# Two repeated gather inputs kept in DRAM, fewer gathers in flight, and a new pace of row steps

## The chip, the cores and the metric

The kernel runs on one core of a Trainium2 chip. A core has a matrix engine (TensorE, PE in the profile), a vector engine (VectorE, DVE), an activation engine (ScalarE, ACT), a general engine (GpSimd, POOL) and a queue engine that only issues DMAs (SyncE, SP). Sixteen DMA engines move data between DRAM (HBM) and the on-chip memory SBUF; TensorE writes to PSUM. Each engine works through its own list of instructions in order and waits on semaphores for the others. The metric is the device time of one execution, in microseconds (us); lower is better.

## What is computed

One layer of a streaming encoder with 512 frames of width 2048 and 16 meta tokens. The first half is attention; it is not touched here. The second half is PEER, a layer with 16384 experts, each one row `u` and one row `v` of 2048 numbers. Every token scores two sets of 128 keys for each of 8 heads, takes the best 16 of each, then the best 16 of the 256 sums, and so has 8 x 16 = 128 experts with weights `g`:

```python
q = (xb @ w_q).reshape(PEER_BLOCK, PEER_HEADS, 2, PEER_HALF)
s = jnp.einsum('thcd,hcnd->thcn', q, sub_keys)
...
h = jnp.einsum('tkd,td->tk', u[idx], xb)
act = (g * jax.nn.gelu(h, approximate=False))
return jnp.einsum('tk,tkd->td', act, v[idx])
```

Everything is float32. A product of two float32 matrices is made of three TensorE products of a high and a low half (`mm3`, lines 259 to 261): low x high, high x low, high x high.

## The kernel before

**Two ways through PEER.** The 512 frames are split. 328 of them (`ND`) go through *all* experts as dense products: a first pass over 128 blocks of `u` (`u_products`), then a second pass over 256 tiles of `v`. The other 184 frames are done with *gathers*: an indirect DMA on GpSimd's queue (line 1042) fetches 128 rows of `u` or `v`, one to each partition (1 MB), and VectorE works on them (a "row step"; line 1055 for `u`, lines 1061 and 1063 for `v`). The 184 frames are four parts, `NS = 128, 32, 16, 8`. For the first each partition holds one frame, and 128 gathers serve its 128 experts. The others have fewer frames than partitions, so each frame's input row is repeated over 4, 8 or 16 partitions, and they take 32, 16 and 8 gathers. That makes 184 row steps on `u` and 184 on `v`. In the list `todo` they stand in one order; the first `NU = 200` are done during the score stage and the first pass, the other 168 during the second pass.

**The repeated inputs.** The inputs of the three small parts are written once to DRAM (`xn_d`, 56 rows, line 1143). `copies(dst, t0, n)` (line 936) reads `n` of these rows so that each is repeated 128/n times, and fills 128 partitions. It is called for part 1 (32 rows) into the tile `xgb`, in the score stage; for part 2 (16 rows) into `lists`, when the routing steps, which use `lists` for their tables, are over; and for part 3 (8 rows) into `lists` again, 8 row steps after parts 0 to 2 are through. All three go out on SP's queue, as do the weight tiles.

**Weight tiles.** `front`, `wtile` and `load` (lines 232 to 256) load a tile of 128 x 1024 (`wr`, four buffers), make its high half on ScalarE (`wh`, line 245) and its low half (`wl`, line 246) on VectorE, or on GpSimd where the call says so. `wh` and `wl` have three buffers; in the first pass and the second there are more.

**The score stage** (lines 1076 to 1174) runs over 16 key sets, here called heads `hc`. Each multiplies the 512 frames by `wq` (two tiles: the first with its low half on VectorE, the second on GpSimd, except for head 1, where both are on VectorE), scales and splits the result, and one head later forms the scores (`scores`) and picks the best 16 on VectorE (`top16`, lines 915 to 919). In head 0 the inputs `xn` of the dense part are normalised, in head 1 they are split into `hgh` and `hgl` (16 splits). At head 4 three gathers are sent, and each head from 5 on does one row step with up to three rows in flight (`row_step(..., 3)`); there are three row buffers (`bufs=3`). Heads 0 and 8 load and split a tile of keys (`skh`, `skl`).

**The first pass** runs over 128 blocks `e`. Each loads two tiles of `u`, makes the dense products of 328 frames (48 matrix instructions), and beside them come the routing of the dense frames (`route`), the gates (`gates_of`) and the row steps. `PACE` says how many row steps are done by which block (linear between its points), and `rows_due` brings the count up to it twice a block. At the turn to the second pass the memory of the first is given back, and one row in four then goes into a buffer that lies there (`gs["pool"]`). In the second pass `PACE_V` does the same over 512 pieces.

The instructions are not run in exactly the order in which they are written: within the dependences a scheduler orders each engine's list, by its own estimate of the times, with what is written earlier first. `add_manual_dep` with `NOSYNC` fixes single orders.

Of the kernel before, what the change touches and what calls it, by code (L numbers as in the profile page):

```python
# [9 lines left out]
F32 = mybir.dt.float32  # L10
# [13 lines left out]
P = 128  # L24
D = 2048
# [10 lines left out]
NK = 128  # L36
# [3 lines left out]
NS = 128, 32, 16, 8  # L40
# [175 lines left out]
def body(tc, nc, a, dbg=None):  # L216
# [73 lines left out]
    gwb_d = dp.tile([NB, P], F32, name="gwb_d")  # L290
    eob_d = dp.tile([NB, P], I32, name="eob_d")
    xn_d = dp.tile([NB, D], F32, name="xn_d")
    h_d = dp.tile([NG, P, GRP, ND], F32, name="h_d")
    g_d = dp.tile([NG, P, NBT, GRP, TH], F32, name="g_d")

# [639 lines left out]
    def copies(dst, t0, n):  # L935
        SP.dma_start(dst, xn_d[t0:t0 + n, None, :].to_broadcast([n, P // n, D]))
# [69 lines left out]


    slots = [[(i, k) for k in range(n)] for i, n in enumerate(NS)]
    NU = 200
    todo = [("u", *s) for i in range(3) for s in slots[i]]  # L1010
    todo += [("v", *s) for s in slots[0][:NU - NR]] + [("u", *s) for s in slots[3]]
    todo += [("v", *s) for s in slots[3] + slots[0][NU - NR:NU - NR + 44] + slots[2] + slots[0][NU - NR + 44:] + slots[1]]
    PACE = (0, 14, 60, 124, NK - 0.5), (11, 26, 94, 194.5, NU)
    PACE_V = (0, 64, 488), (0, 20, 2 * NR - NU)
    OWN = NU - 9
    xs, ys = [xg, xgb, lists, lists], [xg, xgb]
# [30 lines left out]
    def row_step(mark, lead):  # L1047
        n = gs["done"]
        while gs["sent"] < min(len(todo), n + lead):
            send()  # L1050
        (src, part, k), row = todo[n], rows.pop(n)
        w = acts[part][:, k:k + 1]
        if src == "u":
            assert part < 2 or gs["x"] == part
            ins = V.scalar_tensor_tensor(row, row, 1.0, xs[part], ALU.mult, ALU.mult, accum_out=w)  # L1055
        else:
            y = ys[min(part, 2)]
            if part > 1:
                row = row.rearrange("p (c d) -> p c d", d=P)
            if k == 0:  # L1060
                ins = V.tensor_scalar(y, row, w, None, ALU.mult)
            else:
                ins = V.scalar_tensor_tensor(y, row, w, y, ALU.mult, ALU.add)  # L1063
        tc.add_manual_dep(ins.ins, mark.ins.name, NOSYNC, reason="keeps the gathers spread")
        gs["done"] += 1
        if gs["done"] == sum(NS[:3]) + 8:
            gs["x"] = 3
            copies(lists, BO[3], NS[3])
        if src == "u" and k == NS[part] - 1:
            S.activation(acts[part], acts[part], AF.Gelu, scale=rcols[part])  # L1070
            V.tensor_mul(acts[part], acts[part], gws[part])
# [15 lines left out]
    with tc.tile_pool(name="score", bufs=2, side="right") as sp_:  # L1087
        raws = []

        def raw_in():  # L1090
            t = xn.tile([P, ND], F32, name="xn")
            G.dma_start(t, ht_d[len(raws)][:, :ND])
            raws.append(t)

        sk = {}
        def scores(hc, qh, ql):
            ps = ps_tile()
            skh, skl = sk["now"]
            s = slice(hc % 8 * P, (hc % 8 + 1) * P)
            for ti in range(4):  # L1100
                t = slice(ti * P, (ti + 1) * P)
                mm3(ps[:, t], qh[:, t], ql[:, t], skh[:, s], skl[:, s], True, True)
            sc = sp_.tile([P, 4, NK], F32, name="sc")
            S.activation(sc, ps.rearrange("p (t n) -> p t n", n=NK), AF.Copy)
            for ti in (3, 2, 0, 1):
                top16(v1[:, ti, hc], i1[:, ti, hc], sc[:, ti], NK)
            if hc % 4 == 3:
                for _ in range(10):
                    next(early, None)

        late = []
        wq = {(0, hf): front("wq", 0, hf, G if hf else V) for hf in range(2)}
        for _ in range(KC):
            raw_in()
        for hc in range(16):
            ps = ps_tile()
            for hf in range(2):
                wh, wl = wq.pop((hc, hf)) if (hc, hf) in wq else front("wq", hc, hf, G if hf else V)
                for k in range(8):
                    s = slice(k * P, (k + 1) * P)  # L1120
                    kk = hf * 8 + k
                    mm3(ps, wh[:, s], wl[:, s], hgh[:, kk], hgl[:, kk], kk == 0, kk == KC - 1)
                    if (hc, kk) == (0, 3):
                        rstd(rh_, rh_, SEQ, D, sp_, ("qf", "sc", "sc"))
            qh = sp_.tile([P, SEQ], F32R, name="pqh")
            ql = sp_.tile([P, SEQ], F32R, name="pql")
            qf = sp_.tile([P, SEQ], F32, name="qf")
            if hc == 0:


                for hf in range(2):
                    wq[1, hf] = front("wq", 1, hf)
                for m in range(KC):
                    V.scalar_tensor_tensor(raws[m], raws[m], gain("ffn")[:, m:m + 1], rh_[:, :ND], ALU.mult, ALU.mult)
            if hc == 1:
                for m in range(KC):
                    split(hgh[:, m, :ND], hgl[:, m, :ND], raws[m])
                normed.close()
                gs["rows"] = rt.enter_context(tc.tile_pool(name="rows", bufs=3, side="left"))
            V.tensor_mul(qf, ps, rh_)  # L1140
            if hc == 0:
                natural(*last_natural)
                S.dma_start(xn_d, xgb[:NB])
            split(qh, ql, qf)
            late.append((hc, qh, ql))
            if hc == 1:
                V.memset(rh_[:, :ND], 1.0)
            if hc == 4:
                pt_ = ps_tile()
                rr = sp_.tile([P, 4, NK], F32, name="sc")  # L1150
                T.transpose(pt_[:, :P], rh_[:, TA:], ident)
                for j, (t, n) in enumerate(zip(BC[1:], NS[1:])):
                    V.tensor_copy(rr[:, j].rearrange("p (t r) -> p t r", r=P // n), rh_[:, t, None].to_broadcast([P, n, P // n]))
                    T.transpose(pt_[:, (j + 1) * P:(j + 2) * P], rr[:, j], ident)
                V.tensor_copy(rcol, pt_[:, :1])
                for j in range(len(NS) - 1):
                    V.tensor_copy(rcolb[:, j:j + 1], pt_[:, (j + 1) * P:(j + 1) * P + 1])
            if hc:
                scores(*late.pop(0))
            if hc == 1:  # L1160
                copies(xgb, BO[1], NS[1])
            if hc % 8 == 0:
                wr_ = raw_half()
                skh = sp_.tile([P, 1024], F32R, name="skh", bufs=1)
                skl = sp_.tile([P, 1024], F32R, name="skl", bufs=1)
                SP.dma_start(wr_, a["front"][FIDX[("sub", hc // 8, 0)]])
                split(skh, skl, wr_)
                sk["now"] = (skh, skl)
            if hc == 4:
                for _ in range(3):  # L1170
                    send()
            if hc > 4:
                row_step(more["lo"], 3)
        ahead = u_products(0)
        scores(*late.pop(0))

# [152 lines left out]
    for e in range(NK):  # L1329
        g = e // GRP  # L1330
        if e == NK // 2:
            spread_rows()
        if e == NK - 4:
            assert next(steps, steps) is steps and next(gate_steps, steps) is steps
            assert gs["done"] >= OWN
            group_in(0)
        def beside(hf):
            next(gate_steps, None)
            if hf == 0:
                rows_due(e)  # L1340
            for _ in range(hf if e < 8 else 1 if e < 24 or e % 2 else hf):
                if next(steps, steps) is steps and not gs["third"]:
                    gs["third"], gs["x"] = True, 2
                    copies(lists, BO[2], NS[2])

        if e == 0:
            ps = ahead
            for hf in range(2):
                beside(hf)
        else:  # L1350
            ps = u_products(e, beside)
        hb = up.tile([P, ND], F32, name="hb")
        more["gelu"] = S.activation(hb, ps[:, :ND], AF.Gelu)
        S.dma_start(h_d[g][:, e % GRP], hb)
        if e == NK - 2:
            gated(*held[0])
            parts = {0: [vi.tile([P, D], F32R, name=x, tag=t)[:, :GRP * ND].rearrange("p (j t) -> p j t", t=ND)
                         for x, t in (("vah", "gin"), ("val", "hin"))]}
            split(*parts[0], held.pop(0)[0])
        if e == NK - 1:  # L1360
            group_in(1)
        rows_due(e + 0.5)
# [149 lines left out]
```

## Time and profile before

| | us |
|---|---|
| median of 3 runs | 3508.65 |
| lowest, highest | 3507.4, 3513.76 |
| the profiled execution | 3506.72 |
| its span, from first to last instruction | 3504.9 |

The profile is one execution, recorded by the hardware. Its page gives busy time by engine; its views list waits by the engine that waited and what released it, instructions in order of time, the chain of work that ended last, and busy times in windows. In a window's row the clock is the share of full TensorE clock that was granted; PE counts as busy at either clock, so a lower clock has to be counted beside the idle time. The DMA share is the mean busy share of the 16 DMA engines and can pass 1 by a little. Times in rows are us from the start of the span. The score stage runs from about 1317 to 1544, the first pass to about 2546, the second to about 3490.

### The profile page before, as it was taken

What the parts mean: (1) busy time and instruction counts of PE and PEld (TensorE: products, weight loads), DVE (VectorE), ACT (ScalarE), POOL (GpSimd) and SP (SyncE); (2) the same over time, 40 slices, a digit from 0 to 9 for tenths busy, and PEclk for the clock granted to TensorE, in tenths of its full rate; (3) what the DMA queues carried; (4) which work ended last, traced back from release to release, by engine and by line L of the source; (5) the groups of instructions that cost most, each with busy time, mean ns of one, the idle gap of its engine ahead of it and who ended that gap; (6) DMA issues with size and microseconds to landing.
All of it is one profiled execution on the core that took longest, in us unless ns stands there. A gap on an engine that the chain in (4) does not pass through costs nothing.

```text
span 3504.9 us, 53419 instructions
## 1 busy us (share of the span) xinstructions
PE 3435.6 (98%) x21114; PEld 3202.8 (91%) x21114; DVE 2603.3 (74%) x3608; ACT 1420.5 (41%) x2304; POOL 758.1 (22%) x555
## 2 busy tenths in 40 slices
PE   9999999999999999999999999999989999999997
PEld 8988888888888887789999999999989999999997
DVE  5533334346754557999999988887789999999997
ACT  4232233335543223233475676665333333333333
POOL 1000000000011122322233233233212333233330
PEclk9999999999999999999999999999999999999999
DMA  5322222222144434669999999999999999999993
GB/s 172 102 97 97 100 99 94 96 99 79 43 153 138 137 134 136 223 218 338 368 391 395 366 412 412 411 404 359 374 373 367 391 406 401 394 385 398 404 385 124
DMA packets 226854, 917.84 MB, mean 262 GB/s; under 512 B 27775, under 2 KB 53487, under 8 KB 179059
## 3 DMA queue, kind: packets, MB, share of 16 engines
q1 hardware_dynamic: 134372, 464.01, 36.2%
q0 software_dynamic: 60480, 411.68, 29.9%
q10 hardware_dynamic: 31750, 38.75, 3.1%
q8 instruction: 165, 2.70, 0.3%
q14 instruction: 87, 0.70, 0.1%
HBM read 852.47 MB, written 60.81 MB: 261 GB/s over the span
## 4 chain that ended last, share of the span: by engine, by line
PE 63%; DVE 20%; DMA 8%; issue 6%; ACT 1%; POOL 1%; SPq 0%; DVEq 0%; ACTq 0%; POOLq 0%
PE ps L259 20%; PE ps L260 20%; PE ps L261 20%; DVE wl L246 4%; DMA wr<-vb 4%; DVE row L1055 3%; DVE xg L1063 3%; DMA wr<-ut 2%; DVE hgl L246 1%; DVE acc L1482 1%; POOL row L1042 1%; ACT wh L245 1%; DMA g_d<-gb 1%; DVE acc L1063 1%; DMA row<-v,eob 1%
## 5 line engine op out<-in xcount | busy, mean ns | idle before, releaser
L245 ACT ACTIVATE wh<-wr 128x1024 fp32r<-128x1024 f32 (+1 forms) x654 | 687.8, 1053 | 1445.5 <-PE ps L261 1011.6
L246 DVE TENSOR_TENSOR wl<-wr,wh 128x1024 fp32r<-128x1024 f32 (+1 forms) x639 | 812.0, 1279 | 405.8 <-ACT wh L245 404.6
L259 PE MATMUL ps<-vah,wl 128*128 128x328 f32 x2048 | 644.5, 315 | 13.7 <-DVE wl L246 13.2
L260 PE MATMUL ps<-val,wh 128*128 128x328 f32 x2048 | 643.4, 314 | 0.0
L261 PE MATMUL ps<-vah,wh 128*128 128x328 f32 x2048 | 640.5, 313 | 0.0
L259 PE MATMUL ps<-hgh,wl 128*128 128x328 f32 (+1 forms) x1488 | 495.0, 333 | 21.0 <-DVE wl L246 21.0
L261 PE MATMUL ps<-hgh,wh 128*128 128x328 f32 (+1 forms) x1488 | 489.3, 329 | 0.0
L260 PE MATMUL ps<-hgl,wh 128*128 128x328 f32 (+1 forms) x1488 | 489.1, 329 | 0.0
L259 PE MATMUL ps<-xh,wl 128*128 128x512 f32 (+1 forms) x1376 | 468.0, 340 | 1.7 <-ACT xh L365 1.6
L260 PE MATMUL ps<-xl,wh 128*128 128x512 f32 (+1 forms) x1376 | 464.9, 338 | 0.8 <-DVE xl L366 0.8
L261 PE MATMUL ps<-xh,wh 128*128 128x512 f32 (+1 forms) x1376 | 464.9, 338 | 0.0
L259 PEld LDWEIGHTS ps<-vah,wl 128*128 128x128 f32 x2048 | 387.1, 189 | 16.4 <-DVE wl L246 15.6
L260 PEld LDWEIGHTS ps<-val,wh 128*128 128x128 f32 x2048 | 387.9, 189 | 0.0
L261 PEld LDWEIGHTS ps<-vah,wh 128*128 128x128 f32 x2048 | 387.4, 189 | 0.0
L1042 POOL DMA_INDIRECT row<-v,eo x128 | 208.1, 1626 | 501.8 <-DVE xg L1063 421.3
L259 PEld LDWEIGHTS ps<-hgh,wl 128*128 128x128 f32 x1488 | 283.8, 191 | 34.0 <-DVE wl L246 20.2
L1063 DVE SCALAR_TENSOR_TENSOR xg<-row,act,xg 128x2048 f32<-128x2048 f32 x127 | 297.7, 2344 | 4.8 <-DMA row<-v,eo 4.8
L1055 DVE SCALAR_TENSOR_TENSOR row<-row,xg 128x2048 f32<-128x2048 f32 x128 | 295.2, 2306 | 3.1 <-DMA row<-u,eo 3.1
L261 PEld LDWEIGHTS ps<-hgh,wh 128*128 128x128 f32 x1488 | 283.1, 190 | 10.8 <-issue 0.2
L260 PEld LDWEIGHTS ps<-hgl,wh 128*128 128x128 f32 x1488 | 283.7, 191 | 9.8
L259 PEld LDWEIGHTS ps<-xh,wl 128*128 128x128 f32 x1376 | 258.6, 188 | 30.5 <-ACT xh L365 3.4
L260 PEld LDWEIGHTS ps<-xl,wh 128*128 128x128 f32 x1376 | 259.1, 188 | 29.1 <-DVE xl L366 1.7
(512 smaller groups left out, 6081.7 us busy)
## 6 DMA issues: line engine op xcount, KB each, us to landing
wr<-ut SPq DMA_DIRECT2D x256, 512.0 KB
wr<-vb SPq DMA_DIRECT2D x256, 512.0 KB
wr<-front SPq DMA_DIRECT2D x238, 512.0 KB
g_d<-gb POOLq DMA_DIRECT2D x42, 512.0 KB
gin<-g_d SPq DMA_DIRECT2D x32, 672.0 KB
h_d<-hb ACTq DMA_DIRECT2D x128, 164.0 KB
hin<-h_d SPq DMA_DIRECT2D x32, 656.0 KB
gates<-gt ACTq DMA_DIRECT2D x32, 256.0 KB
```

Of the source, the lines that this page charges most:

```text
L245: more["last"] = S.activation(hi[:, s], r, AF.Copy)
L246: sub = (eng or V).tensor_sub(lo[:, s], r, hi[:, s].bitcast(F32))
L259: T.matmul(ps, wl, xh, start=start, stop=False)
L260: T.matmul(ps, wh, xl, start=False, stop=False)
L261: T.matmul(ps, wh, xh, start=False, stop=stop)
L1042: G.indirect_dma_start(out=row, out_offset=None, in_=a[src], in_offset=bass.IndirectOffsetOnAxis(ap=eos[part][:, k:k + 1], axis=0))
L1055: ins = V.scalar_tensor_tensor(row, row, 1.0, xs[part], ALU.mult, ALU.mult, accum_out=w)
L1063: ins = V.scalar_tensor_tensor(y, row, w, y, ALU.mult, ALU.add)
L1482: mark = V.tensor_add(acc[:, c, :ND], acc[:, c, :ND], ps[:, :ND])
```

## The change

```diff
+    xr_d = dp.tile([2, P, D], F32, name="xr_d")
...
-    NU = 200
+    NU = 198
...
-    PACE = (0, 14, 60, 124, NK - 0.5), (11, 26, 94, 194.5, NU)
+    PACE = (0, 14, 60, NK - 0.5), (11, 26, 94, NU)
...
         if gs["done"] == sum(NS[:3]) + 8:
             gs["x"] = 3
-            copies(lists, BO[3], NS[3])
+            SP.dma_start(lists, xr_d[1])
...
             if hc == 1:
+                wq[2, 0] = front("wq", 2, 0)
                 for m in range(KC):
                     split(hgh[:, m, :ND], hgl[:, m, :ND], raws[m])
...
-            if hc == 1:
+            if hc == 6:
                 copies(xgb, BO[1], NS[1])
+            if hc in (9, 12):
+                copies(xr_d[hc // 3 - 3], BO[hc // 3 - 1], NS[hc // 3 - 1])
...
             if hc == 4:
-                for _ in range(3):
+                for _ in range(2):
                     send()
             if hc > 4:
-                row_step(more["lo"], 3)
+                row_step(more["lo"], 2)
...
                     gs["third"], gs["x"] = True, 2
-                    copies(lists, BO[2], NS[2])
+                    SP.dma_start(lists, xr_d[0])
```

- A new DRAM tile `xr_d` holds two filled inputs of 128 x 2048. At heads 9 and 12 of the score stage `copies` writes parts 2 and 3 into it, from DRAM to DRAM. Where `copies` filled `lists` in the first pass, a plain load from `xr_d` stands now.
- The copy for part 1 is written at head 6 instead of head 1.
- The first weight tile of head 2 is requested in head 1, ahead of the 16 splits.
- In the score stage two rows are in flight instead of three.
- 198 row steps instead of 200 come before the second pass, which has 170 instead of 168. From block 60 on the pace is one straight line, from 94 to 198 over 67.5 blocks, instead of 94 to 194.5 over 64 and on to 200.

## The prediction

> **What bounds the kernel now.** I read the page first, then TensorE's waits, then windows round each wait.
>
> ```profile
> span 3504.9 us, 53419 instructions
> ...
> PE 3435.6 (98%) x21114; PEld 3202.8 (91%) x21114; DVE 2603.3 (74%) x3608; ACT 1420.5 (41%) x2304; POOL 758.1 (22%) x555
> ```
>
> TensorE (PE) is busy for 98% of the span, so an edit gains only where PE stands still. The waits of PE say for whom:
>
> ```profile
> PE ps L259 <- DVE wl L246: 34.2, 15, 7.2
> ...
> PE ps L260 <- DVE skl L265: 2.5, 1, 2.5
> ```
>
> Nearly all of it is the low half of a weight tile that VectorE (DVE) delivers late (line 246), 34.2 us in 15 waits. The windows show where, and a second price (columns: window, its length, busy us and count of PE, weight loads, DVE, ACT, POOL, then granted clock, DMA share, GB/s).
>
> ```profile
> 1338.00:1352.00 14.00, 9.46 (x40) 7.76 (x39) 13.91 (x44) 5.55 (x11) 4.00 (x1) 0.76 0.35 123
> 1420.00:1432.00 12.00, 9.09 (x40) 7.38 (x39) 11.86 (x42) 2.22 (x4) 4.46 (x3) 0.86 0.86 307
> 1448.00:1462.00 14.00, 11.52 (x44) 9.57 (x43) 13.69 (x54) 2.17 (x3) 0.38 (x1) 0.76 0.41 141
> 1954.00:1968.00 14.00, 11.34 (x67) 10.79 (x67) 9.75 (x17) 10.04 (x25) 1.61 (x1) 0.88 1.03 407
> 1983.00:1997.00 14.00, 10.74 (x59) 10.46 (x58) 13.79 (x19) 9.57 (x22) 4.56 (x4) 0.76 0.83 248
> 2000.00:2390.00 390.00, 390.00 (x2814) 384.84 (x2813) 337.64 (x374) 265.05 (x638) 131.19 (x106) 1.00 1.02 410
> 2416.00:2430.00 14.00, 10.10 (x56) 9.72 (x55) 8.01 (x7) 6.72 (x15) 1.44 (x2) 0.76 0.97 358
> 2474.00:2486.00 12.00, 9.25 (x53) 8.98 (x52) 7.18 (x5) 6.18 (x8) 1.70 (x2) 0.86 0.94 336
> 2544.00:2560.00 16.00, 8.78 (x45) 8.51 (x45) 12.91 (x11) 1.34 (x2) 4.58 (x3) 0.79 0.99 409
> 2720.00:3440.00 720.00, 718.03 (x4778) 717.08 (x4776) 673.99 (x569) 239.75 (x222) 234.33 (x134) 1.00 0.98 389
> ```
>
> A stall costs its idle time plus the clock that is lost after it: length minus PE busy, plus (1 - clock) times length. For the first: 14 - 9.46 = 4.5, plus 0.24 x 14 = 3.4, **7.9 us**. Likewise 4.6 (1420), 5.8 (1448), **4.4** (1954), 6.6 (1983), **7.3** (2416), 4.4 (2474) and 10.6 (2544). In 2000 to 2390 PE has no idle time at all, and in 2720 to 3440 it has 2 us, with the DMAs at 410 and 389 GB/s: there is little to gain there, and something to lose.
>
> **The change part by part.** (a) *The early tile for `wq[2,0]`* meets the stall at 1338. VectorE and GpSimd (POOL) there, with ScalarE (ACT):
>
> ```profile
> 1328.98 1.07 ACT L245 ACTIVATE wh<-wr 128x1024 fp32r<-128x1024 f32 x1 [4.43 <-PE ps L261]
> ```
>
> ```profile
> 1337.21 5.41 DVE L265 TENSOR_TENSOR hgl<-xn,hgh 128x328 fp32r<-128x328 f32 x13
> 1342.55 0.68 DVE L1140 TENSOR_TENSOR qf<-ps,rh__9389 128x512 f32<-128x512 f32 x1
> 1343.15 2.76 DVE L246 TENSOR_TENSOR wl<-wr,wh 128x1024 fp32r<-128x1024 f32 x1
> ```
>
> ```profile
> 1340.84 4.00 POOL L246 TENSOR_TENSOR wl<-wr,wh 128x1024 fp32r<-128x1024 f32 x1 [10.81 <-ACT wh L245]
> ```
>
> ```profile
> 1080.00:1120.00 40.00, 40.00 (x178) 33.14 (x177) 19.90 (x18) 14.16 (x18) 5.17 (x4) 1.00 0.41 136
> ```
>
> The high half that belongs to the DVE piece at 1343.15 was there at 1330 (same load semaphore), but its low half came behind 13 of the 16 splits of `hgh` (5.41) and `qf`. Made ahead of the splits it is done near 1338, before PE asks for it (1345.9, where the piece ends, less the 4.5 of idle time: 1341.4). No work is added; the splits and `qf` end one such piece later, and `scores(1)`, which wants them, comes only after the 11 us of products for head 2 (48 of 512 columns; the row shows 178 such in 40 us). The second half of head 2 is POOL's piece, done at 1344.84, when PE has 5.5 us of the first half to do from 1341.4: covered. I take the whole 7.9 (bounds 4.5 and 7.9).
>
> (b) *The repeated rows.* Today `copies` reads 16, then 8, rows of `xn_d` again and again into the 128 partitions of `lists`.
>
> ```profile
> 1936.33 0.57 SPq L936 DMA_DIRECT2D lists<-xn_d  x1
> ```
>
> ```profile
> 2389.24 0.66 SPq L936 DMA_DIRECT2D lists<-xn_d  x1
> ```
>
> ```profile
> 1924.00:1940.00 16.00, 16.00 (x117) 15.78 (x117) 15.97 (x31) 10.17 (x27) 3.60 (x3) 1.00 1.03 408
> 1940.00:1952.00 12.00, 12.00 (x91) 11.78 (x90) 10.49 (x13) 5.37 (x13) 5.33 (x5) 1.00 1.03 281
> 2380.00:2396.00 16.00, 16.00 (x117) 15.78 (x116) 10.81 (x13) 10.85 (x30) 3.59 (x3) 1.00 1.04 411
> 2396.00:2416.00 20.00, 20.00 (x149) 19.67 (x148) 8.69 (x7) 7.04 (x17) 4.63 (x4) 1.00 1.01 242
> ```
>
> The share stays full while the rate falls from 408 to 281 and from 411 to 242 GB/s: the repeats make every packet slower. Lost: 127 x 12 = 1.5 MB, or 3.7 us of DMA time, and 169 x 20 = 3.4 MB, or 8.2 us. The weight loads stand behind on SP's queue:
>
> ```profile
> 1938.94 17.82 DMA wr<-ut
> ```
>
> ```profile
> ACT wh L245 <- DMA wr<-ut: 16.7, 2, 15.1
> ```
>
> The first row is the chain at the 16-row copy, the second ACT's waits from 2385 to 2425; they are the stalls at 1954 and 2416. After the change each place issues one ordinary load of 1.05 MB, two weight tiles' worth: 2.6 us at 409 GB/s, instead of some 12 and 20. The four `wr` buffers hold two blocks, of 7 to 8 us each (128 of them from about 1540 to 2546), and hide that, so I take both stalls as gone: 4.4 + 7.3 = **11.7** (bounds 0 and 11.7; at the lower one half the cover fails each time). The stall at 1983 stays: DVE is in the last pieces of routing there, which the diff doesn't touch.
>
> The copies themselves move to the score stage, DRAM to DRAM. No such DMA stands in the trace. Its nearest rows are the 32-row copy, which stays, and the score stage:
>
> ```profile
> 1337.00:1341.00 4.00, 4.00 (x24) 3.46 (x23) 4.00 (x11) 4.00 (x10) 0.17 (x1) 1.00 0.61 238
> 1440.00:1540.00 100.00, 96.75 (x477) 82.64 (x476) 95.78 (x336) 26.69 (x35) 21.00 (x13) 0.97 0.44 150
> ```
>
> ```profile
> 1335.40 0.62 SPq L936 DMA_DIRECT2D xgb<-xn_d  x1
> 1344.86 16.89 SPq L243 DMA_DIRECT2D wr<-front  x5
> ```
>
> At 0.44 share there is room. Written in the code for heads 6, 9 and 12, they may go out sooner, since SP issues what is ready:
>
> ```profile
> L931 SPq DMA_DIRECT2D gwb<-gwb_d x3: 327/442/447, 1656.7 to 1658.0; - x3
> ```
>
> That line is written at block 64 of 128, half way through a stage of 1540 to 2546, and went out some 380 us before that. Bounds: nothing, or twice 7.3 if each copy starves PE as the worst one does today. I take nothing: the weight loads of this stage run four tiles ahead, one tile per 5.5 to 6 us, about 20 us. If the cover fails, the weights of heads 4 and 5 are late.
>
> (c) *Two rows in flight in the score stage.*
>
> ```profile
> 1409.24 2.29 DVE L1055 SCALAR_TENSOR_TENSOR row<-row,xg 128x2048 f32<-128x2048 f32 x1 [0.81 <-DMA row<-u,eo]
> ...
> 1413.11 4.22 DVE L1055 SCALAR_TENSOR_TENSOR row<-row,xg 128x2048 f32<-128x2048 f32 x1 [1.57 <-DMA row<-u,eo]
> ```
>
> ```profile
> 1411.81 0.94 POOL L1042 DMA_INDIRECT row<-u,eo  x1 [4.86 <-DVE row L1055]
> 1412.77 2.40 POOL L246 TENSOR_TENSOR wl<-wr,wh 128x1024 fp32r<-128x1024 f32 x1
> ```
>
> With three buffers and three rows ahead, POOL waits 4.86 for the row before to be used, and its weight piece stands behind that wait; it then runs beside DVE's row step, which takes 4.22 instead of 2.29. With two ahead a buffer is always free. Gone from DVE's line: 0.81 + 1.57 + 1.93 = **4.3 us**. DVE is at 95.78 of 100 us in this stage and sets the stalls at 1420 and 1448 (10.4 together), so DVE's time is what counts. I take 4.3 (bounds: 10.4 gained, or 5 lost if later rows arrive late by as much as the 0.8 and 1.6 above, three or four times).
>
> (d) *198 rows instead of 200 in the first pass, at an even pace.* Two row steps move to the second pass:
>
> ```profile
> L1063 DVE SCALAR_TENSOR_TENSOR xg<-row,act,xg 128x2048 f32<-128x2048 f32 x127 | 297.7, 2344 | 4.8 <-DMA row<-v,eo 4.8
> ```
>
> That is 2 x 2.34 us of DVE, which has 46 us of slack in 2720 to 3440, and 2 x 1.05 MB, 5.4 us at 389 GB/s or nothing if hidden. The pace falls from 100.5/64 = 1.570 rows a block to 104/67.5 = 1.541, which eases the stalls at 2474 and 2544 by as much at best. I take 1 us lost (bounds 5.4 either way).
>
> Sum: -7.9 - 11.7 - 4.3 + 1.0 = **-22.9**. The profiled execution took 3506.7 us (1.8 outside the span), so 3483.8; the median lies 1.9 above it: **3486 us**.
>
> TensorE: Matmul & The Clock Gate of the Trainium skill (Part 1, the HAM clock gate) says that the clock halves after an idle window of about 3.4 us. The window at 1448 lost 24% of its clock after 2.5 us of idle time, so the trace does not hold to that. By that rule only the waits at 1338 and 2416 would lose clock, and the sum would be smaller by the 1.7 us of the 1954 window: 3488.
>
> **The rivals.** *The second read is no better* (the change doesn't do what it says): 1 MB in front of the weight tiles delays them whatever its source. For it: the queue is saturated there (1.03 and 1.04). Against: the rate fell only while rows were repeated. Gained: 7.9 + 4.3 - 1, so 3497. Chance 0.13.
>
> *DVE takes its part back*: at 95.78 of 100 us in the score stage it may give back (c) and the clock part of (a), 7.7 us: 3494. Chance 0.12.
>
> *The copies starve the score stage* (slower): they stand on SP's queue in front of the weight loads. If all three go out near 1336, loads issued from 1344.86 on, for head 4 at about 1366, wait behind them. At the speed of today's two, 12 + 20 us, they end near 1373; with DRAM on both sides they may take twice that, 64 us, ending near 1405, and PE would stand some 35 to 40 us. It decides from about 22 us of copy on, and makes the kernel slower by 0.2% (7 us) when the wait is over 22.9 + 7 = 30 us, so from some 52 us on: 3508.7 - 22.9 + 40 = 3526. Against it: 238 GB/s for the 32-row copy, 4 us. Chance 0.13.
>
> **How the numbers follow.** The forecast holds 0.62, with its own range 3474 to 3497 (from -35 to -12, the bounds of c and d). The range reaches up into the rivals and to a partial starving: 3470 to 3509. A measurement can tell about 0.2%, 7 us, from no change. Faster: the forecast and the first two rivals, less what misses the bound: 0.75. Within 0.2%: 0.12, where starving eats the gain. Slower: 0.13.
>
> **What would show it.** Right: PE at or near 14.00 with clock 1.00 in the windows that replace 1338, 1954 and 2416; about 400 GB/s or more through both `lists` loads; no 4.86 us wait of POOL on L1055 near 1411. Wrong: long `wr<-front` DMAs in the chain between 1335 and 1510; PE waits of 2 us and more after either `lists` load; more than 5 us of PE idle time in the second pass; or a stall at the turn of the passes well above 10.6, since POOL's first gather into memory that the first pass frees is now the third row of that pass.

## The result, and the profile after

| | us | ratio to before, 95% interval |
|---|---|---|
| before, median of 4 runs | 3508.03 | |
| after, median of 4 runs (3482.83 to 3487.11) | 3486.82 | 0.9934, 0.9917 to 0.9951 |
| profiled execution after, its span | 3486.89, 3485.1 | |

The change makes the kernel faster by 0.66% (0.49 to 0.83%), some 23 us by the ratio; the same kernel run again later (r7, below) has 0.9949. The page of the changed kernel:

```profile
span 3485.1 us, 53427 instructions
## 1 busy us (share of the span) xinstructions
PE 3429.8 (98%) x21114; PEld 3196.8 (92%) x21114; DVE 2602.1 (75%) x3608; ACT 1420.2 (41%) x2304; POOL 770.9 (22%) x555
```

Every engine has as many instructions as before; PE stands still less often. Its waits for the low halves of the weight tiles fell from 34.2 us to

```profile
PE ps L259 <- DVE wl L246: 20.6, 12, 4.2
```

The windows of the changed kernel that answer to those of before (window, length, busy us and count of PE, weight loads, DVE, ACT, POOL, then clock, DMA share, GB/s):

```profile
1338.00:1352.00 14.00, 14.00 (x70) 11.80 (x69) 13.98 (x44) 9.12 (x18) 6.21 (x2) 1.00 0.63 234
1420.00:1432.00 12.00, 10.39 (x52) 8.41 (x50) 11.86 (x35) 2.92 (x4) 9.55 (x5) 1.00 0.74 265
1441.00:1455.00 14.00, 10.25 (x41) 8.54 (x40) 13.69 (x58) 2.17 (x3) 1.81 (x1) 0.76 0.53 187
1951.00:1965.00 14.00, 14.00 (x104) 13.78 (x103) 12.15 (x28) 10.44 (x26) 2.56 (x2) 1.00 1.03 413
1977.00:1991.00 14.00, 9.78 (x54) 9.38 (x54) 13.79 (x19) 9.74 (x22) 4.57 (x4) 0.76 0.80 255
2410.00:2424.00 14.00, 14.00 (x100) 13.89 (x99) 11.58 (x10) 7.65 (x17) 4.29 (x3) 1.00 1.02 420
2457.00:2471.00 14.00, 14.00 (x96) 14.00 (x95) 11.18 (x8) 7.13 (x9) 2.26 (x2) 1.00 0.93 364
2526.00:2542.00 16.00, 11.79 (x69) 11.53 (x68) 12.18 (x9) 2.12 (x2) 3.65 (x2) 0.89 1.01 408
2858.00:2872.00 14.00, 11.02 (x63) 10.76 (x62) 12.34 (x11) 4.19 (x4) 8.39 (x3) 0.88 1.00 397
```

Counted as in the prediction (length minus PE busy, plus the clock that is missing), in the order of the rows: the stall at 1338 is gone (-7.9); the one at 1420 fell from 4.6 to 1.6; the one at the second key tile grew from 5.8 to 7.1; the stall behind the 16-row copy is gone (-4.4); the one at 1983 grew from 6.6 to 7.6; the stall behind the 8-row copy is gone (-7.3). Then come three that the prediction did not have: the stall at 2474 is gone too (-4.4), the one at the turn of the passes fell from 10.6 to 6.0, and a new one of 4.7 stands at 2861.

The following table splits each profiled span by TensorE's own instructions: up to the first product of `scores(0)`, to the last product of `scores`, to the first product of the second pass, and to its last product. In brackets stand PE's idle time (gaps over 0.3 us) and the time lost to a lower clock. The stall "at the turn" lies in the fourth column. The run names are those of the experiments below.

| | front part | score stage | first pass | second pass |
|---|---|---|---|---|
| before | 1340.0 | 199.9 (10.7 + 8.5) | 988.5 (18.4 + 10.2) | 958.7 (13.5 + 8.5) |
| after | 1342.8 | 191.0 (6.1 + 3.4) | 977.6 (11.2 + 5.1) | 955.7 (11.6 + 5.1) |
| e1: (a) alone | 1339.7 | 192.5 (5.8 + 5.1) | 991.6 (20.1 + 10.2) | 955.6 (9.0 + 10.2) |
| e2: (b) alone | 1341.8 | 200.1 (10.4 + 8.5) | 974.5 (10.7 + 3.4) | 952.7 (8.9 + 6.8) |
| e3: (c) alone | 1338.5 | 196.9 (10.2 + 6.8) | 985.9 (17.7 + 6.8) | 957.9 (13.4 + 10.2) |
| e4: (d) alone | 1341.6 | 200.2 (10.1 + 8.5) | 985.1 (17.0 + 5.1) | 955.7 (12.1 + 6.8) |
| r5: (a), (b), (c) | 1339.8 | 190.3 (5.6 + 3.4) | 975.2 (9.7 + 3.4) | 954.6 (9.4 + 6.8) |
| r6: (a), (b) | 1339.5 | 193.0 (6.3 + 5.1) | 972.2 (8.9 + 1.7) | 954.6 (11.9 + 5.1) |
| r7: changed, again | 1341.3 | 190.6 (5.7 + 3.4) | 971.2 (8.1 + 1.7) | 958.3 (14.0 + 5.1) |
| r8: r5 + early keys | 1341.9 | 188.6 (4.8 + 1.7) | 973.1 (8.9 + 3.4) | 958.6 (11.3 + 10.2) |
| s9: outer repeat | 1341.7 | 200.5 (10.7 + 8.5) | 985.6 (19.4 + 8.5) | 963.8 (13.7 + 15.4) |
| s10: distinct rows | 1341.8 | 199.9 (10.4 + 8.5) | 974.6 (9.4 + 3.4) | 953.1 (8.7 + 8.5) |
| s11: r5, even pace | 1338.5 | 190.9 (6.0 + 3.4) | 971.4 (8.4 + 1.7) | 951.3 (9.6 + 5.1) |
| s12: r8, GpSimd | 1339.9 | 191.4 (6.4 + 3.4) | 973.3 (9.3 + 3.4) | 952.6 (10.0 + 5.1) |

Every run has the same front part, and it varies by 4 us: single spans don't tell 3 us apart. A stage is compared with the same stage, and totals by their ratios.

The three copies, two of them from DRAM to DRAM, went out early, as the prediction had guessed. SP's queue in the timeline of the changed kernel, and the landing times of the DMA view (count, KB each, median us from issue to landing):

```profile
1339.80 0.62 SPq L937 DMA_DIRECT2D xgb<-xn_d  x1
1340.47 0.58 SPq L937 DMA_DIRECT2D xr_d<-xn_d  x1
1348.80 0.33 SPq L243 DMA_DIRECT2D wr<-front  x1
1349.19 0.75 SPq L937 DMA_DIRECT2D xr_d<-xn_d  x1
```

```profile
xr_d<-xn_d SPq DMA_DIRECT2D x2, 1024.0 KB, 8.6
```

Written for heads 6, 9 and 12, they were issued in heads 1 and 2, some 54, 92 and 126 us before those heads begin in this trace (at 1393.5, 1432.2 and 1475.5). Each copy into `xr_d` took 8.6 us (the second by its last packet), and the last packet of the three ended 18 us after the first issue (12 us in e2, where all three go out together). That is below the 22 us of copy at which the starving rival would have begun, though not by much.

### The profile page after: what moved, and what is told of

Read it like the earlier page. It is cut to its first block, busy times and chain, and to the rows that moved or that the text cites. A ratio compares the mean times of both kernels' runs of the same rounds, so it can differ in the third digit from the quotient of the medians.

```text
span 3485.1 us, 53427 instructions
## 1 busy us (share of the span) xinstructions
PE 3429.8 (98%) x21114; PEld 3196.8 (92%) x21114; DVE 2602.1 (75%) x3608; ACT 1420.2 (41%) x2304; POOL 770.9 (22%) x555
## 4 chain that ended last, share of the span: by engine, by line
PE 67%; DVE 18%; DMA 8%; issue 5%; ACT 2%; POOL 0%; SPq 0%; DVEq 0%; ACTq 0%; POOLq 0%
PE ps L259 21%; PE ps L260 21%; PE ps L261 21%; DVE wl L246 4%; DVE row L1056 3%; DMA wr<-ut 3%; DMA wr<-vb 3%; DVE xg L1064 2%; DVE hgl L246 1%; ACT wh L245 1%; DMA g_d<-gb 1%; PE ps L1238 1%; DVE acc L1486 1%; DVE acc L1064 1%; DMA row<-u,eo 1%
## 5 line engine op out<-in xcount | busy, mean ns | idle before, releaser
L259 PE MATMUL ps<-vah,wl 128*128 128x328 f32 x2048 | 644.1, 314 | 12.0 <-DVE wl L246 11.3
L259 PEld LDWEIGHTS ps<-vah,wl 128*128 128x128 f32 x2048 | 386.3, 189 | 15.4 <-DVE wl L246 14.4
L259 PEld LDWEIGHTS ps<-hgh,wl 128*128 128x128 f32 x1488 | 281.7, 189 | 23.7 <-DVE wl L246 11.6
## 6 DMA issues: line engine op xcount, KB each, us to landing
g_d<-gb POOLq DMA_DIRECT2D x42, 512.0 KB, 11.6
```

The source lines that it names most:

```text
L259: T.matmul(ps, wl, xh, start=start, stop=False)
```

## The experiments

### The four parts, one at a time on the kernel before

e1 is (a) alone.

```diff
             if hc == 1:
+                wq[2, 0] = front("wq", 2, 0)
```

> Only (a), the early tile for wq[2,0], on the kernel before. Theory: the stall at 1338 (4.5 us of idle time and 3.4 us of clock) goes and nothing else moves: the stretch from scores(0) to the last scores falls from 198.7 to about 190.8, the time by 7.9 us, ratio 0.9977. Rival (DVE takes its part back): DVE is the bound of the score stage, the stalls at 1420 and 1448 (10.4 together) grow by part of it, and only 2 to 4 us are gained.

Measured: ratio 0.9971 (0.9960 to 0.9981), so -10 us (7 to 14). The score stage is 7.4 us shorter (the table's count ends 1.2 us later than the 198.7 of the expectation). Windows of e1:

```profile
1335.00:1349.00 14.00, 14.00 (x70) 11.80 (x69) 13.98 (x46) 9.12 (x18) 6.40 (x2) 1.00 0.44 151
1405.00:1417.00 12.00, 9.63 (x37) 7.51 (x36) 11.62 (x31) 2.06 (x3) 10.55 (x5) 0.86 0.78 289
1440.00:1454.00 14.00, 11.32 (x44) 9.45 (x43) 13.69 (x56) 2.17 (x3) 0.71 (x1) 0.76 0.47 169
```

PE is full in the first; the stalls in the other two are 4.1 and 6.0, where they were 4.6 and 5.8. The rival, that DVE takes its part back, is out for (a).

e2 is (b) alone: the lines of the diff with `xr_d`, and the places of the copies.

```diff
-            copies(lists, BO[3], NS[3])
+            SP.dma_start(lists, xr_d[1])
...
-                    copies(lists, BO[2], NS[2])
+                    SP.dma_start(lists, xr_d[0])
```

> Only (b), the repeated rows written to DRAM in the score stage and read back by two plain loads, on the kernel before. Theory: the stalls at 1954 (4.4) and 2416 (7.3) go, the score stage stays within 1 us, the stalls at 2474 (4.4) and at the turn of the passes (10.6) stay: -11.7, ratio 0.9967. Rival (lost DMA time): the 12 us of DMA time that the repeats cost are also what makes the DMAs late at 2474 and at the turn, so that those stalls shrink too, as they did in the full change: about -20, ratio 0.994. If the copies disturb the score stage, scores(0) to the last scores is over 200 us.

Measured: 0.9952 (0.9936 to 0.9967), so -17 us (12 to 22), more than the 11.7 of the two stalls. The score stage is the same to 0.2 us: the DRAM copies are hidden. Windows of e2 behind both loads, at the former 2474, and at the turn:

```profile
1952.00:1966.00 14.00, 13.47 (x94) 13.11 (x93) 10.68 (x21) 8.80 (x24) 2.71 (x3) 1.00 1.02 403
2410.00:2424.00 14.00, 14.00 (x104) 13.78 (x103) 12.00 (x11) 10.54 (x26) 4.18 (x3) 1.00 1.02 409
2458.00:2472.00 14.00, 14.00 (x96) 14.00 (x95) 7.34 (x6) 4.89 (x6) 0.94 (x1) 1.00 1.02 418
2532.00:2548.00 16.00, 11.24 (x63) 10.98 (x62) 11.84 (x12) 3.38 (x4) 3.65 (x2) 0.79 1.01 416
```

The third row is the one that the theory had wrong: the stall of 4.4 is gone, although the two loads of the first group go out as close together as before (SP's queue, timeline of e2):

```profile
2450.37 0.33 SPq L1304 DMA_DIRECT2D gin<-g_d  x1
2450.80 0.40 SPq L243 DMA_DIRECT2D wr<-ut  x1
2451.36 0.33 SPq L1312 DMA_DIRECT2D hin<-h_d  x1
```

Before they went out at 2463.71 and 2464.68. The DMAs run at a share of about 1.0 there, so what the 8-row copy made late was still late 60 us on. Run s9 below bears that out: there the 8-row copy gets shorter, the 16-row copy does not, and PE is busy for all of 2460 to 2500. The stall at the turn falls from 10.6 to 8.1 as well. The rival (lost DMA time) holds for 2474, and in part for the turn.

e3 is (c) alone.

```diff
-                for _ in range(3):
+                for _ in range(2):
                     send()
             if hc > 4:
-                row_step(more["lo"], 3)
+                row_step(more["lo"], 2)
```

> Only (c), two rows in flight instead of three in the score stage, on the kernel before. The prediction had -4.3 us. From the full change: the stall at 1420 falls from 4.6 to about 1.6 and the one at the second key tile (skl, 1448) rises from 5.8 to about 7, so -1.7 net, ratio 0.9995. Rival: the shift at skl came from the rest of the change, and both stalls shrink here, -4 us or more.

Measured: 0.9986 (0.9978 to 0.9995), so -5 us (2 to 8); the score stage is 3.0 us shorter. Windows of e3:

```profile
1424.00:1436.00 12.00, 10.89 (x55) 8.89 (x54) 11.69 (x43) 3.13 (x4) 7.98 (x5) 1.00 0.88 303
1443.00:1457.00 14.00, 10.22 (x41) 8.59 (x40) 13.69 (x59) 2.17 (x3) 1.47 (x1) 0.76 0.50 179
```

1.1 and 7.1 us: the shift to the key tile, as in the full change. POOL's timeline in the changed kernel shows why the gain is small:

```profile
1402.25 0.94 POOL L1043 DMA_INDIRECT row<-u,eo  x1 [0.30 <-issue]
1403.20 2.40 POOL L246 TENSOR_TENSOR wl<-wr,wh 128x1024 fp32r<-128x1024 f32 x1
1409.55 3.02 POOL L1043 DMA_INDIRECT row<-u,eo  x1 [3.96 <-DVE row L1056]
```

The third gather is sent at once, now in front of the weight piece, and POOL still waits for DVE's row before it has a buffer for the fourth, 3.96 us instead of 4.86. What changed is that the weight piece no longer stands behind that wait. The pace of DVE is what it was.

e4 is (d) alone.

```diff
-    NU = 200
+    NU = 198
...
-    PACE = (0, 14, 60, 124, NK - 0.5), (11, 26, 94, 194.5, NU)
+    PACE = (0, 14, 60, NK - 0.5), (11, 26, 94, NU)
```

> Only (d), 198 rows in the first pass at the new pace, on the kernel before. The prediction had +1.0 us. Theory now: with 198 rows the two loads hin and gin of the first group, which went out back to back near 2464, stand apart on SP's queue, so the stall at 2474 (4.4) goes and the one at the turn falls from 10.6 to about 6, while the second pass gets a new stall of about 4.7 near 2860: -4 us in all, ratio 0.9988, with the stall of 7.3 behind the 8-row copy still there. Rival (lost DMA time, from b): the stalls at 2474 and at the turn stay as they were, and the time rises by 1 to 5 us.

Measured: 0.9981 (0.9969 to 0.9992), so -7 us (3 to 11). Windows of e4: at the 8-row copy, which goes out at 2407.75, at the former 2474, at the turn, and in the second pass:

```profile
2408.00:2420.00 12.00, 12.00 (x87) 11.89 (x86) 11.95 (x12) 8.26 (x24) 6.71 (x5) 1.00 0.92 208
2474.00:2486.00 12.00, 9.24 (x61) 8.79 (x60) 6.87 (x4) 4.20 (x6) 0.00 (x0) 1.00 1.01 409
2543.00:2559.00 16.00, 10.04 (x51) 9.77 (x50) 13.70 (x12) 2.73 (x4) 6.87 (x3) 0.79 1.00 402
2874.00:2888.00 14.00, 11.70 (x78) 11.43 (x77) 12.01 (x12) 4.40 (x5) 7.53 (x2) 1.00 1.01 410
```

The stall at 2474 stays (2.8) and the turn has 9.3, so the theory on the two group loads falls. The gain comes from a place that nobody named: the 8-row copy, later by the new pace, runs at 208 GB/s and costs PE nothing there. Alone, (d) hides the copy that (b) removes. With (b) in place that gain can't be had twice.

### What (c) and (d) are worth with the rest in place

Four runs side by side. r5 is the changed kernel without (d):

```diff
-    NU = 198
+    NU = 200
...
-    PACE = (0, 14, 60, NK - 0.5), (11, 26, 94, NU)
+    PACE = (0, 14, 60, 124, NK - 0.5), (11, 26, 94, 194.5, NU)
```

> The changed kernel without (d): 200 rows in the first pass and the old pace, (a), (b) and (c) kept. Theory: with (b) in place (d) has nothing left to gain and costs some 5 us, 2 to 3 of them as the wait near 2861 of the second pass and the rest in the first pass, so this is about 4 to 5 us faster than the changed kernel: ratio to before about 0.9925 (the changed kernel 0.9934 to 0.994), second pass about 953 us. Rival: (d) is what shrank the stalls at 2474 and at the turn in the changed kernel; without it they come back and this is 4 to 9 us slower than the changed kernel.

r6 is r5 with three rows in flight again (e3's diff taken back):

> Only (a) and (b) on the kernel before: three rows in flight, 200 rows, the old pace. Theory: (a) and (b) act in different stages and add up, 7.6 + 17.8 us by the spans of the two alone, so about -25, ratio 0.993; beside the run without (d) it tells what (c) is worth once (a) is there: 1.7 to 3 us. Rival: DVE is the bound of the score stage, so of (a) and (c) together only one is worth its time, and this run and the one without (d) are equal within 1 us.

r7 is the changed kernel itself, with no edit:

> The changed kernel once more, beside the others: 0.9934 as before, within 0.002, score stage 190 to 191 us, second pass about 955 us with the wait near 2861.

| | median us | ratio to before |
|---|---|---|
| r5 | 3478.87 | 0.9921 (0.9908 to 0.9934) |
| r6 | 3481.07 | 0.9934 (0.9921 to 0.9947) |
| r7 | 3486.15 | 0.9949 (0.9936 to 0.9961) |

r5 is 7 us faster than r7, and their intervals don't meet: **(d) costs time once the other three parts are there**, and the version without it beats both kernels. r5 against r6 gives (c) 2 us in the median, which their intervals can't tell from none, and 2.7 us in the score stage.

s11 splits (d): it keeps the even pace and goes back to 200 rows.

```diff
-    NU = 198
+    NU = 200
```

> The changed kernel with NU = 200 again, but with the new even pace from block 60. It splits (d): without both parts 3479, with both 3486. Theory: the two rows that 198 moves into the second pass are the cost (two more row steps, and another order of the v rows there), the even pace is worth about nothing: ratio 0.992, second pass without the wait near 2860. Rival: the even pace is the cost: ratio 0.994 to 0.995, as in the changed kernel.

Measured: 3479.58 us, 0.9930 (0.9916 to 0.9943). The median lies beside r5's, which speaks for the two rows as the cost, but it is not shown: the interval takes in the rival's 0.994 and meets r7's. Where the time goes is clear in part. One PE wait of 2.3 to 3.0 us stands near 2860 in all three profiles with 198 rows (the changed kernel, r7 and e4); in the other eleven no wait for `wl` between 2600 and 3410 is over 1.8 us, s11 with its even pace among them, so this wait belongs to the two rows. The whole second pass says less: 955.7 and 958.3 us in the two profiles of the changed kernel, 954.6 and 951.3 in r5 and s11, but 958.6 in r8, also with 200 rows. DVE's timeline of the changed kernel at the new stall:

```profile
2854.39 1.22 DVE L246 TENSOR_TENSOR wl<-wr,wh 128x1024 fp32r<-128x1024 f32 x1
2855.52 2.34 DVE L1064 SCALAR_TENSOR_TENSOR acc<-row,actb,acc 128x2048 f32<-128x2048 f32 x1
2857.78 0.48 DVE L1486 TENSOR_TENSOR acc<-acc,ps 128x328 f32<-128x328 f32 x1
2858.19 2.34 DVE L1064 SCALAR_TENSOR_TENSOR acc<-row,actb,acc 128x2048 f32<-128x2048 f32 x1
2860.45 0.48 DVE L1486 TENSOR_TENSOR acc<-acc,ps 128x328 f32<-128x328 f32 x1
2860.86 2.34 DVE L1064 SCALAR_TENSOR_TENSOR acc<-row,actb,acc 128x2048 f32<-128x2048 f32 x1
2863.12 4.62 DVE L246 TENSOR_TENSOR wl<-wr,wh 128x1024 fp32r<-128x1024 f32 x4
```

Three row steps on `acc` stand between one weight piece and the next, and then four pieces have piled up (x4); in r5 at most two stand there (at 2835.91 and 2838.58). At the turn 198 rows do gain: about 6 in both profiles of the changed kernel, 8 in r5. Where the rest of the 7 us lies stays open: r7's profile is of its fastest execution (3480.85), r5's of its slowest (3479.60), so the two hardly differ.

### What makes the copies slow

s9 repeats the rows in another order.

```diff
-            copies(lists, BO[3], NS[3])
+            outer(lists, BO[3], NS[3])
...
+    def outer(dst, t0, n):
+        SP.dma_start(dst, xn_d[None, t0:t0 + n, :].to_broadcast([P // n, n, D]))
```

> The kernel before, with the two copies into lists written with the repeat outermost: all 16 (or 8) rows once, then all again, 8 (or 16) times over. The rows land in other partitions, so parts 2 and 3 get the inputs of other frames of theirs: that assignment is left out. Bytes, rows and packets are the same. Theory (the same few DRAM rows are read again and again, in whatever order): the rate stays at 240 to 290 GB/s while the copies run, the stalls at 1954 and 2416 stay, ratio 1.000. Rival (the order decides: with the rows outermost a 16-way split of the 8-row copy would not come out even; the section on how many engines a transfer gets, in DMA: Bandwidth & Descriptors of the Trainium skill, would give the 8-row copy 8 engines before and 16 here, and the 16-row copy 16 before and 8 here): the stall of 7.3 at 2416 goes and the one at 1954 (4.4) stays or grows, about -5, ratio 0.9985.

Measured: 0.9997 (0.9987 to 1.0008). That is the theory's total, but not its stalls. Windows of the kernel before, over the slow stretch of the 16-row and of the 8-row copy (from the first 8 KB packet after the issue that took over 0.42 us to the last, where most take 0.31):

```profile
1941.00:1953.00 12.00, 12.00 (x91) 11.78 (x90) 9.49 (x13) 4.56 (x13) 5.33 (x5) 1.00 1.02 278
2393.00:2417.00 24.00, 24.00 (x176) 23.67 (x175) 8.84 (x8) 10.04 (x27) 4.92 (x5) 1.00 1.02 271
```

And of s9, with the stall that follows the first:

```profile
1942.00:1962.00 20.00, 16.95 (x121) 16.29 (x120) 12.83 (x15) 6.28 (x15) 5.34 (x5) 1.00 1.03 299
1956.00:1974.00 18.00, 7.68 (x42) 7.01 (x41) 6.14 (x13) 5.62 (x14) 1.83 (x2) 0.72 0.93 330
2403.00:2421.00 18.00, 18.00 (x131) 17.78 (x130) 8.69 (x7) 9.68 (x26) 4.86 (x4) 1.00 1.02 327
```

The stretch of the 16-row copy grew from 12 to 20 us and its stall from 4.4 to 15.4 (18 - 7.68 + 0.28 x 18); that of the 8-row copy fell from 24 to 18, and its stall is gone. So both are at work. The rate falls in either order, to 271 to 327 GB/s where the plain loads of s10 (below) have 419 and 422: repeated rows are slow to read here. The copies' own packets of 8 KB take 0.54 and 0.55 us in the median before, 0.49 and 0.48 in s9, and 0.31 in s10. Repetition alone doesn't do it: in the score stage, where the queue had room, the packets of the two copies into `xr_d` also take 0.31 us. Why repeated rows slow down beside a full load, no run here shows. And the order sets how long it lasts: the long stretch belongs to the copy whose outer dimension is 8. Counted by the copies' own packets alone, the 16-row copy goes from 11 to 16 us and the 8-row copy from 21 to 12. DMA: Bandwidth & Descriptors of the Trainium skill (on why a DMA increments its semaphore by 16) says that a transfer gets the largest number of engines, up to 16, that divides the slowest dimension of both sides. By that the slow copies have 8 engines, and the runs agree: 24 and 20 us with an outer 8, 12 and 18 with an outer 16. Which engine moved a packet the trace doesn't say, but the packets that run at once fit: of the copy's own at most 7 and 8 with an outer 8 (the 8-row copy before, the 16-row copy of s9), up to 15 and 13 with an outer 16. In e4 the 8-row copy has 8 at once for 6.4 of its 14 us and up to 10 for moments.

s10 leaves repetition out.

```diff
-            copies(lists, BO[3], NS[3])
+            SP.dma_start(lists, a["u"][:P])
...
-                    copies(lists, BO[2], NS[2])
+                    SP.dma_start(lists, a["u"][P:2 * P])
```

> The kernel before, with both copies into lists replaced by a plain load of 128 different rows of u (the same 1.05 MB, the same places in the code); nothing is copied in the score stage. The repeated inputs are left out: parts 2 and 3 multiply with rows of u. Theory (repetition is the cost, not the volume): 400 GB/s and more through both loads, no stall at 1954, 2416 or 2474, last scores to the second pass about 974 us as with the plain lists loads alone, ratio about 0.995. Rival (1 MB in front of the weight tiles is the cost): the stalls stay at 4 to 7 us each, ratio 0.999 to 1.000.

Measured: 0.9961 (0.9945 to 0.9976), 3489.85 us beside e2's 3490.53. Windows of s10 from the issue of each load:

```profile
1940.00:1952.00 12.00, 12.00 (x91) 11.78 (x90) 12.00 (x20) 7.22 (x16) 5.10 (x4) 1.00 1.01 419
2388.00:2400.00 12.00, 12.00 (x91) 11.78 (x90) 6.83 (x10) 8.34 (x22) 1.88 (x2) 1.00 1.02 422
```

The same 1.05 MB at the same place, at full rate. Its volume costs nothing, and the rival "the second read is no better" is out.

### Two attempts at the score stage

r8 is r5 with the second key tile made ahead, in a second pair of buffers.

```diff
+            if hc == 7:
+                key_tile(1)
             if hc:
                 scores(*late.pop(0))
...
-                skh = sp_.tile([P, 1024], F32R, name="skh", bufs=1)
-                skl = sp_.tile([P, 1024], F32R, name="skl", bufs=1)
+            skh = sp_.tile([P, 1024], F32R, name="skh")
+            skl = sp_.tile([P, 1024], F32R, name="skl")
```

> The changed kernel without (d), and with the second key tile (skh, skl) loaded and split from head 7 on, in buffers of its own, so that TensorE finds it when scores(8) begins. Theory: the wait of 3.75 us at skl and its 3.4 us of clock go and DVE does no more work than before: 5 to 7 us faster than the run without (d). Rival: DVE is busy for about 96% of the score stage, so the time saved at skl comes back as waits for wl or at the last scores; then it gains less than 2 us.

Measured: 3478.00 us, 0.9923 (0.9911 to 0.9935), beside r5's 3478.87. The wait at `skl` is gone, yet the score stage is only 1.7 us shorter. Windows of r8:

```profile
1400.00:1440.00 40.00, 37.19 (x176) 31.22 (x175) 37.93 (x131) 8.93 (x12) 19.22 (x12) 0.96 0.77 290
1440.00:1540.00 100.00, 96.71 (x507) 83.72 (x507) 98.28 (x355) 26.55 (x34) 21.54 (x13) 1.00 0.48 166
```

Of the first 40 us 2.8 are idle, and in the next 100 DVE has 98.28. The rival holds: the gain is under 2 us, and the wait went elsewhere. From 1400 to 1540 PE waits 5.4 us for `wl` in r8, where r5 has 3.8 for `skl` and 1.3 for DVE's `wl`.

s12 takes five weight pieces off DVE.

```diff
-                wh, wl = wq.pop((hc, hf)) if (hc, hf) in wq else front("wq", hc, hf, G if hf else V)
+                wh, wl = wq.pop((hc, hf)) if (hc, hf) in wq else front("wq", hc, hf, G if hf or hc in (6, 8, 10, 12, 14) else V)
```

> The run with the early key tile, and the low half of the first wq tile of heads 6, 8, 10, 12 and 14 on GpSimd instead of VectorE: five pieces of 1.2 to 2.8 us, some 10 us, less on DVE. Theory (DVE is the bound of the score stage, which is why the early key tile gained nothing): what was given back there shows now: scores(0) to the last scores falls from 188.6 to 184 to 186, the time by 3 to 4 us, ratio 0.991. Rival: GpSimd's pieces of 2.4 to 4 us come late instead, or slow DVE's steps beside them: 188 to 192 us, ratio 0.992 to 0.993.

Measured: 3484.75 us, 0.9940 (0.9926 to 0.9954), the score stage 191.4. The same view of s12, and DVE and POOL at the end of PE's longest wait there (5.4 us, up to 1456.96):

```profile
1440.00:1540.00 100.00, 92.93 (x473) 80.34 (x473) 96.68 (x353) 25.13 (x33) 27.61 (x15) 0.97 0.46 160
```

```profile
1454.00 2.81 DVE L265 TENSOR_TENSOR pql<-qf,pqh 128x512 fp32r<-128x512 f32 x1
```

```profile
1453.92 2.34 POOL L246 TENSOR_TENSOR wl<-wr,wh 128x1024 fp32r<-128x1024 f32 x1 [12.19 <-ACT wh L245]
```

The theory's gain doesn't come, and the rival holds in its second half: no GpSimd piece is late, but GpSimd's pieces slow DVE's steps beside them. PE waits for `pql`, whose split takes 2.81 us beside GpSimd's piece and 0.68 at most other heads. Two more take 2.46 and 2.05 us, again beside such a piece; in r8 all three take 0.68. DVE is nearly as full as before. Neither attempt beats r5.

## Why the prediction was right, and where it was not

- **The time.** 3486 was forecast and 3486.8 measured. A hit that close is luck in part, for errors cancel: (b) gave more, (c) a little less, and (d) cost seven times its term.
- **(a), -7.9.** Right: 7.9 by the windows, 7.4 in the score stage of e1.
- **(b), -11.7.** Both stalls went, the DRAM copies are hidden, and no stall came in their place. The term was too small: e2 gained 17 us. The step that failed is that (b) was priced by its two own windows alone; the stalls at 2474 and 2544 appear only in (d), as something that the pace may ease. DMA time lost near 2400 was still missing at 2474 (4.4 gone), and in part at the turn (2.5 in e2). The reason given, that repeats make every packet slower, is half of it: in s9 the order of the dimensions alone takes the 8-row copy from 21 to 12 us and the 16-row copy from 11 to 16.
- **(c), -4.3.** The direction was right, the size too large: 3.0 in e3, 2.7 on top of (a) and (b). DVE time was counted at 1420 and 1448 alike; the wait at the key tile grew by 1.3. "With two ahead a buffer is always free" was wrong: POOL still waits 3.96 us.
- **(d), +1.0, at most 5.4 either way.** Wrong in size, and outside its bound: about +7 with the other parts in place, and -7 alone. "46 us of slack in 2720 to 3440" is an average. The row steps on `acc` near 2855 come in a cluster, where DVE had no room, and PE waited 3.0 us; the rest of the 7 is open. The sign "more than 5 us of PE idle time in the second pass" could not tell, for by the table the kernel before has 13.5.
- **The rivals.** "DVE takes its part back" came true for (c) in part and in r8; not for (a). The starving copies and the slow second read did not come.

## What to carry to other kernels

A load that reads few rows many times on a full queue costs DMA time by its repetition and by its split over the engines, not by its bytes: write the repeated form to DRAM where the queue has room, and read it plainly where it is full. On a full queue lost time shows up again later, so a removed stall can be worth more than its own window. Parts of a change that repair the same stall don't add up: try each with and without the others, for one of them (here the 198 rows) may be a loss by now.

## What the runs showed of the hardware

- **A lower clock with PE counted as busy.** Windows of the changed kernel, and a line of PE's timeline:

```profile
3098.00:3102.00 4.00, 4.00 (x34) 4.00 (x34) 3.72 (x3) 1.06 (x1) 0.94 (x1) 0.91 1.00 413
3102.00:3106.00 4.00, 4.00 (x21) 4.00 (x20) 4.00 (x5) 1.06 (x1) 0.94 (x1) 0.66 1.03 422
```

```profile
3097.72 3.64 PE L1388 MATMUL ps<-select,acc 128*128 128x16 f32 x32
```

  PE counts as busy throughout, and the clock falls to 0.91 and 0.66. But for 3.6 us before that it makes only narrow products, 32 of 16 columns, where the others have 328. Ten of the other thirteen profiles of this study have such a dip near that place. Each profile has three such groups, of 8, 16 and 32 columns; in 23 of the 42 the clock falls within 1.5 us of the group's end.
- **The clock follows fixed steps of time, not the length of the pause alone.** In the changed kernel 4.2 us of idle time lost 3.4 us of clock at 1977 and 1.7 at the turn; in e1 2.4 us lost 1.7 (clock 0.86 in 1405 to 1417). In all 14 profiles the lower clock is one half, and each of its 112 stretches begins on a grid of 3.413 us steps that is fixed within a profile (to 2 ns) and lasts whole steps. Between 1310 and 3440 take the steps at full clock, and count in each the time in which PE was idle or in one of the narrow groups above. Under 1.75 us, half clock followed in 3 of 8482 steps; from 1.75 to 2 us in 11 of 20; over 2 us in 84 of 87. So about half a step is enough, and where a pause lies on the grid decides what it costs. The pause of 2.4 us in e1 is short of the idle window of about 3.4 us in TensorE: Matmul & The Clock Gate of the Trainium skill (Part 1, the HAM clock gate), as was that at 1448 before; by these counts the window need not be idle as a whole.
- **DRAM-to-DRAM copies with repeated rows were quick where the queue had room:** 8.6 us each from issue to landing, for copies that the prediction had priced at up to twice 12 and 20.
